# Low keys on both partition halves: a full-height second score matmul, and duplicated key loads as two DMAs of 64 rows

## Chip, cores and metric

The kernel runs on one core of one Trainium2 chip. The metric is the device time of one launch in microseconds. Shown are the median and the ends of three runs, and one further execution that the hardware profiler recorded.

## What is computed

One inference step of a two-layer streaming encoder, for a prompt of 1024 positions (one sequence) and for 8 x 16 sample positions that attend to cached keys and values. Layer 0 uses sliding-window attention with 4 key heads shared by 16 query heads, learned sinks and a T5 bias; layer 1 uses a band of 9 chunks of 64 positions, 16 heads, and a key and value projected once from the residual stream. Each attention is followed by an output projection, a normalisation, and a gated MLP with a causal convolution. The part that matters here is the attention over the prompt:

```python
def band_attend(q, k, v, qpos, kpos, bias, sinks, n_back):
    ...
    s = jnp.einsum('bqkgd,bskd->bkgqs', qg, k).astype(jnp.float32) * ATTN_SCALE
    s = s + bias.reshape(KV, G, Lq, Lk).astype(jnp.float32)
    ...
        p = jax.nn.softmax(s, axis=-1)
    ...
    o = jnp.einsum('bkgqs,bskd->bqkgd', p.astype(v.dtype), v)
```

Head dimension is 64, so one score has 64 products. Everything is float32.

## The kernel before

Nearly all matmuls run on pairs of numbers: a value is split into a high part, rounded to the matmul's input type, and a low part, the rest. A product is then formed as high x high + high x low + low x high. For the weight matmuls (the functions `mmT`, line 266, and `mmX`, line 278) that is three matmuls of 128 rows for each block.

The program is straight-line code: key and value projections, attention, output projection (`out_proj`) and MLP (`ffn`) for each of the two layers. Attention works through 16 heads (8 column blocks c of two halves a) and, for each head, four pairs g of query tiles with 128 queries each. `work` lists these 64 pairs. For each pair, `scores` forms the scores, `softmax` takes a minimum on VectorE (line 471) and an exponential on ScalarE (line 475), `weigh` transposes the probabilities on TensorE (line 533) and splits them (lines 538, 539), and `values` multiplies them with the values (line 552). These run one to three pairs apart, and between them stand blocks of the next query projection (`qblock`, line 266), steps of the adaptive-norm weights (`ada`, line 210, in layer 0) and the items of the sample positions (lines 619, 654). A scheduler orders the instructions of the five engines from its own model of time; each engine then takes its instructions in order. All DMAs are issued in order from SyncE's queue, SP.

A query tile holds 64 dimensions on 128 partitions: the high part on one half (r), the low part on the other. The high keys of a head (`khi[a]`, 64 rows of 1024 positions) lie on both halves, so that one matmul of 128 rows (line 505) gives high query x high key + low query x high key. The low keys (`klo`, one tile for both halves a) lie on one half only, and a second matmul of 64 rows (line 510) adds high query x low key into the same accumulator. In layer 0 a query tile sees 128 or 256 keys, in layer 1 128 to 640; over 512 they are split into two pieces. Over both layers there are 320 such pieces.

`kload(c, a)` brings the keys and values of a head from DRAM: line 433 fills both halves of `khi[a]` with one DMA whose source is read twice (a leading dimension of 2 with stride 0), line 434 brings the 64 low rows, line 435 the values. It is called 20 times: twice ahead of each layer's loop, and in `finish`, once a head's last values are formed, 14 times in layer 1 and twice in layer 0.

Buffers: `pts` is a ring of eight tiles for the split, transposed probabilities (four in X2, four in the weight slots 2 and 3). The weight slots are four pairs of tiles `wh`, `wl`; in attention the query weights use slots 0 and 1, and just ahead of it the projections use all four. `out_proj` loads its eight blocks of weights ahead, into the weight slots and into parts of the tile that held keys, values and queries (`x1att`), through two staging tiles `ws` (line 164), ScalarE (line 149) and GpSimd or VectorE (line 160).

Of the kernel before, what the change touches and what calls it, by code (L numbers as in the profile page):

```python
# [10 lines left out]
F32 = mybir.dt.float32  # L11
# [76 lines left out]
class Trunk:  # L88
# [249 lines left out]
    def attention(self, l, wk):  # L338
        nc, I = self.nc, self.I
# [4 lines left out]
        self.X1 = self.x1p.tile([128, 9216], F32R, name=f"x1att{l}", tag="x1")  # L344
        xa = Arena(self.X1)
        khi = [xa.take(1024) for _ in range(2)]
        klo = xa.take(1024)
        vst = [xa.take(1024).rearrange("p (k d) -> p k d", d=128) for _ in range(2)]
        qst = [[xa.take(1024) for _ in range(2)] for _ in range(2)]

        def qs(c, a, r, t0, n):
            if c == 7:
                return self.H[r, a, 0, t0 : t0 + n]
            return qst[c % 2][a][r, t0 : t0 + n]

        x2 = Arena(self.X2)
        pts = [(x2.take(512), x2.take(512)) for _ in range(4)]
        pts += [(w[:, 0:512], w[:, 512:1024]) for s in self.wslots[2:4] for w in s]
        pts = Ring(pts)
        fa = Arena(self.F)  # L360
        sKt = fa.take(2176)
# [28 lines left out]
        def head_of(c, a):  # L390
            return 8 * (c // 4) + 4 * a + c % 4 if l == 0 else 2 * c + a
# [24 lines left out]
        for p in range(2):  # L416
            t = sb.next()[:, 0:KS]
# [9 lines left out]
            sbt.append(t)  # L427

        def kload(c, a):
            r = slice(64 * a, 64 * a + 64)  # L430
            row = c * 128 + 64 * a
            kh, kl = kH[0, row : row + 64, :], kH[1, row : row + 64, :]
            nc.sync.dma_start(khi[a].bitcast(F32), bass.AP(kh.tensor, kh.offset, [[0, 2], [1024, 64], [1, 1024]]))
            nc.sync.dma_start(klo[r, :].bitcast(F32), kl)
            nc.sync.dma_start(
                vst[a].bitcast(F32), vH[:, 2 * c + a, :].rearrange("(k p) d -> p k d", p=128)
            )
# [29 lines left out]
        def softmax(pieces, p, n, sink, nm, rs):  # L467

            init = 3.0e38 if sink is None else sink
            for ps, b, c0, w in pieces:  # L470
                nc.vector.tensor_tensor_reduce(  # L471
                    out=p[:, c0 : c0 + w], in0=ps, in1=b, scale=1.0, scalar=init, op0=ALU.add, op1=ALU.min, accum_out=nm
                )
                init = nm
            nc.scalar.activation(p[:, 0:n], p[:, 0:n], AF.Exp, bias=nm, scale=-1.0, accum_out=rs)

        def scores(x):
            c, a, g = x.head.c, x.head.a, x.g
            hh = 2 * c + a
            h = head_of(c, a)  # L480
            r = slice(64 * a, 64 * a + 64)
            if g == 0:
                x.head.b = bias.next()
                nc.sync.dma_start(x.head.b, bass.AP(base.tensor, base.offset + h * HS + 127, [[EW - 1, 128], [1, W]]))
                nc.gpsimd.memset(x.head.b[0:64, W - 64 : W], BIG)  # L485
                nc.gpsimd.memset(x.head.b[64:128, 0:64], BIG)
            x.p = []
            for qi in (2 * g, 2 * g + 1):
                k0 = max(0, qi - back)
                n = (qi + 1 - k0) * 128  # L490
                p = pring.next()
                bo = W - n
                widths = [n] if n <= 512 else [n // 2, n // 2]
                pieces, c0 = [], 0
                for w in widths:
                    first = l == 1 or qi == 2 * g
                    if first:
                        s = self.bank(sbk.next())
                    o = s[:, 0:w] if first else s[:, 256 : 256 + w]
                    kc = slice(k0 * 128 + c0, k0 * 128 + c0 + w)  # L500
                    kw = {"skip_group_check": True} if l == 0 else {}
                    with ExitStack() as es:
                        if not first:
                            es.enter_context(self.tc.issue_after(lead))
                        mm = nc.tensor.matmul(  # L505
                            o, qs(c, a, slice(0, 128), qi * 128, 128), khi[a][:, kc], start=first, stop=False, **kw
                        )
                    if first:
                        lead = mm.ins
                    nc.tensor.matmul(o, qs(c, a, r, qi * 128, 128), klo[r, kc], start=False, stop=True, **kw)  # L510
                    pieces.append((o, x.head.b[:, bo + c0 : bo + c0 + w], c0, w))
                    c0 += w
                i = hh * 8 + qi
                nm = M[:, i : i + 1] if l == 0 else self.sm.next()[:, 0:1]
                softmax(pieces, p, n, self.sink[:, h : h + 1] if l == 0 else None, nm, L[:, i : i + 1])
                x.p.append((p, k0))
# [179 lines left out]
        def finish(i):  # L696
            x = work[i]
            values(x)
            if x.g == 3:
                c, a = x.head.c, x.head.a  # L700
                if l == 1 and c < 7:
                    kload(c + 1, a)
                elif l == 0 and c == 3:
                    kload(1, a)
            if i == 6 * 8 - 1:
                sums(0)

        for a in range(2):
            kload(0, a)
# [5 lines left out]
        for i, x in enumerate(work):  # L715
            scores(x)
            for c, bi in QAT.get(i, ()):
                if bi is None:
                    qload(c)
                else:  # L720
                    qblock(c, bi, qw[c])
            if i >= lw:
                weigh(work[i - lw])
            if i >= lag:
                finish(i - lag)
            self.step(BGA)
            if not self.bg and len(sbk.items) == 4:
                sbk.items = [0, 1, 2, 3, 4]
            for _ in range(ITEMS.count(i)):
                steps += items.pop(0)  # L730
            for _ in range(min(len(steps), 1 + (len(steps) > 4) + (len(steps) > 8))):
                steps.pop(0)()
# [616 lines left out]
```

## Time and profile before

| | us |
|---|---|
| median of 3 runs | 3238.45 |
| lowest, highest | 3228.12, 3243.93 |
| the profiled execution | 3225.61 |
| its span | 3223.7 |
| TensorE busy | 3004.9 (93%) |
| weight loads of TensorE | 2606.3 (81%) |
| VectorE busy | 1519.0 (47%) |
| ScalarE busy | 1137.0 (35%) |
| GpSimd busy | 830.6 (26%) |
| DMA, moved | 367.54 MB |

Times in the views count from the start of the span. PE is TensorE's matmul row, PEld its weight loads, DVE VectorE, ACT ScalarE, POOL GpSimd, SPq the queue of DMA issues. A row of the timeline gives start, duration, engine, line, operation, tiles, shape and count; in brackets the idle time of the engine ahead of it and what ended it ("issue" where the profile shows nothing that it waited for). A row of the chain gives start, duration and the piece of work on the path that ended last. PEclk is the granted clock of TensorE as a share of full speed.

The attention of layer 0 lies at about 125 to 435 us, that of layer 1 at about 1770 to 2190 us. The long stretches of `ffn` lie between and behind them.

### The profile page before, as it was taken

Reading aid. Unit: us, or ns where it says so; the run is one execution under the profiler, and the core shown is the slowest. Engines: PE = TensorE matmul, PEld = TensorE weight load, DVE = VectorE, ACT = ScalarE, POOL = GpSimd, SP = SyncE. Lnnn points to the kernel's source line nnn. Section 1 sums busy time; section 2 is a strip of 40 time slices with the busy share of each in tenths; the row PEclk is TensorE's granted clock in tenths of the full one; section 3 lists DMA queues with packets and bytes.
Section 4 is the critical chain, followed back from the end, with each engine's and each line's share of the span. In section 5 each row is a group of like instructions: output and inputs, shape, how many; then the busy total and the mean of one; then the engine's idle time right before and its main releaser. Section 6 shows DMA issues by size and latency. Waiting matters only on the chain.

```text
span 3223.7 us, 42690 instructions
## 1 busy us (share of the span) xinstructions
PE 3004.9 (93%) x16524; PEld 2606.3 (81%) x16524; DVE 1519.0 (47%) x3162; ACT 1137.0 (35%) x2400; POOL 830.6 (26%) x599
## 2 busy tenths in 40 slices
PE   7799976999999999998899999987699999999996
PEld 4676755888888888897899877755589999999996
DVE  4244556724444443458213545545662444444458
ACT  3254632432222222224335555542244222222224
POOL 2001202422222222254451000000242222222243
PEclk8898987999999999999999999977899999999999
DMA  7334467532222222223685245458531111111122
GB/s 287 126 113 143 142 161 153 196 128 74 79 77 87 87 82 85 83 85 126 225 272 170 89 120 156 131 150 185 126 133 42 46 40 48 41 40 40 40 72 81
DMA packets 226035, 367.54 MB, mean 114 GB/s; under 512 B 34448, under 2 KB 148944, under 8 KB 225448
## 3 DMA queue, kind: packets, MB, share of 16 engines
q1 hardware_dynamic: 225832, 364.81, 36.6%
q8 instruction: 130, 2.13, 0.3%
q14 instruction: 73, 0.60, 0.1%
HBM read 289.40 MB, written 84.79 MB: 116 GB/s over the span
## 4 chain that ended last, share of the span: by engine, by line
PE 71%; DMA 12%; DVE 7%; SPq 3%; POOL 2%; issue 2%; ACT 2%; DVEq 0%; ACTq 0%; POOLq 0%
PE PS L266 41%; PE PS L1057 15%; PE PS L552 3%; PE PS L510 3%; PE PS L210 3%; PE PS L533 2%; PE PS L278 2%; PE PS L505 2%; DMA x1att<-rD 1%; DMA F<-rD 1%; DMA F<-zd 1%; DMA ws<-in_wo_dram 1%; DMA X<-oT 1%; DMA oT<-F 1%; DMA F<-xd 1%
## 5 line engine op out<-in xcount | busy, mean ns | idle before, releaser
L266 PE MATMUL PS<-H,wh 128*128 128x384 f32 (+1 forms) x5472 | 1057.8, 341 | 0.3 <-DVE H L160 0.3
L266 PEld LDWEIGHTS PS<-H,wh 128*128 128x128 f32 x5472 | 973.2, 190 | 20.6 <-issue 9.1
L266 PE MATMUL PS<-H,wl 128*128 128x384 f32 (+1 forms) x2736 | 576.3, 348 | 41.7 <-DVE X L327 13.5
L986 DVE SCALAR_TENSOR_TENSOR F<-PS,F 128x256 f32<-128x256 f32 (+2 forms) x704 | 353.0, 512 | 532.9 <-ACT F L983 519.5
L160 POOL TENSOR_TENSOR wl<-ws,wh 128x1024 fp32r<-128x1024 f32 x167 | 407.4, 2445 | 741.5 <-ACT wh L149 722.3
L266 PEld LDWEIGHTS PS<-H,wl 128*128 128x128 f32 x2736 | 493.4, 192 | 84.8 <-issue 37.5
L1057 PE MATMUL PS<-wh,X 128*128 128x512 f32 x1584 | 466.8, 394 | 12.8 <-DVE acc L1048 4.3
L983 ACT ACTIVATE F<-PS,F 128x384 f32<-128x384 f32 x264 | 177.4, 672 | 756.7 <-PE PS L266 755.3
L1057 PEld LDWEIGHTS PS<-wh,X 128*128 128x128 f32 x1584 | 294.2, 188 | 75.5 <-issue 9.2
L1048 DVE TENSOR_TENSOR acc<-acc,PS 128x512 f32<-128x512 f32 x324 | 221.5, 686 | 273.1 <-PE PS L1057 272.1
L1032 POOL TENSOR_TENSOR F<-F 128x384 f32<-128x384 f32 x132 | 138.1, 1046 | 642.5 <-ACT F L1030 640.6
L1057 PE MATMUL PS<-wl,X 128*128 128x512 f32 x792 | 246.8, 393 | 0.0
L278 PE MATMUL PS<-wh,H 128*128 128x256 f32 (+1 forms) x1008 | 198.8, 327 | 35.8 <-DVE H L160 27.7
L149 ACT CAST wh<-ws 128x1024 fp32r<-128x1024 f32 x176 | 182.1, 1045 | 132.5 <-PE PS L1057 76.9
L278 PEld LDWEIGHTS PS<-wh,H 128*128 128x128 f32 x1008 | 154.8, 199 | 51.7 <-DVE H L160 29.3
L1057 PEld LDWEIGHTS PS<-wl,X 128*128 128x128 f32 x792 | 149.3, 189 | 33.0
L160 DVE TENSOR_TENSOR X<-F,X 128x384 fp32r<-128x384 f32 x132 | 116.8, 885 | 101.6 <-ACT X L149 101.1
L533 PE MATMUL PS<-C,F 128*128 128x128 f32 x720 | 127.9, 294 | 14.2 <-DVE X L539 10.3
L471 DVE CUSTOM_DVE_ANT_0 F<-PS,F,C 128x256 f32<-128x256 f32 (+3 forms) x208 | 98.1, 481 | 80.7 <-PE PS L510 63.1
L485 POOL MEMSET F<- 64x64 f32 x32 | 4.6, 144 | 470.2 <-DMA F<-skb 250.9
L160 POOL TENSOR_TENSOR H<-F,H 128x1024 fp32r<-128x1024 f32 x23 | 58.4, 2537 | 248.2 <-ACT H L149 155.4
L471 DVE CUSTOM_DVE_ANT_0 F<-PS,F 128x320 f32<-128x320 f32 (+5 forms) x144 | 67.7, 481 | 109.2 <-PE PS L533 67.1
(192 smaller groups left out, 3310.2 us busy)
## 6 DMA issues: line engine op xcount, KB each, us to landing
ws<-in_wup_dram SPq DMA_DIRECT2D x88, 512.0 KB
F<-in_adaw_dram SPq DMA_DIRECT2D x74, 512.0 KB
ws<-in_wdn_dram SPq DMA_DIRECT2D x44, 512.0 KB
ws<-in_adaw_dram SPq DMA_DIRECT2D x32, 512.0 KB
X<-oT SPq DMA_DIRECT2D x64, 256.0 KB
xd<-F SPq DMA_DIRECT2D x27, 512.0 KB
F<-xd SPq DMA_DIRECT2D x27, 512.0 KB
x1att<-kH SPq DMA_DIRECT2D x20, 512.0 KB
```

The costliest lines, as they stand in the source:

```text
L149: nc.scalar.copy(out, in_)
L160: self.eng(el).tensor_sub(lo, src, hi.bitcast(F32))
L210: nc.tensor.matmul(ps[32 * j : 32 * j + 32, :], self.cT[:, k * 32 : k * 32 + 32], w[:, j2 * 512 : j2 * 512 + 512], start=k == 0, stop=k == ...
L266: self.nc.tensor.matmul(out[:, 0:n], w[a][:, k * 128 : k * 128 + 128], H[:, p, k, s0 : s0 + n], start=i == 0, stop=i == 23)
L278: self.nc.tensor.matmul(out[:, 0:n], H[:, p, j * kn + k, t0 : t0 + 128], w[a][:, k * n : k * n + n], start=i == 0, stop=i == 23,)
L471: nc.vector.tensor_tensor_reduce(out=p[:, c0 : c0 + w], in0=ps, in1=b, scale=1.0, scalar=init, op0=ALU.add, op1=ALU.min, accum_out=nm)
L533: nc.tensor.transpose(t[:, m * 128 : m * 128 + 128], p[:, (kt - k0) * 128 : (kt - k0) * 128 + 128], self.ident)
L983: nc.scalar.activation(y, ps[:, off : off + 384], AF.Identity, bias=w(3), scale=w(2))
L986: nc.vector.scalar_tensor_tensor(o, u, w(i), o, op0=ALU.mult, op1=ALU.add)
L1032: nc.gpsimd.tensor_mul(a, y, ya[bi])
L1048: nc.vector.tensor_add(row[:, n], row[:, n], ps)
L1057: nc.tensor.matmul(ps, ac[m][p][:, cs], w[m][q][:, n], start=i == 0, stop=i == 5)
```

## The change

The low keys get a tile for each half a: the first stays where `klo` was, the second is the low tile of weight slot 3, which leaves the ring `pts`. Each tile holds the 64 rows twice, on both partition halves, like the high keys. The second score matmul takes the same 128-row query tile as the first, so it adds low query x low key as well. In `kload` every half of every key tile is a DMA of its own, from 64 rows to 64 partitions: four key DMAs per call instead of two, and 512 KB of low keys instead of 256 KB.

```diff
-        klo = xa.take(1024)
+        klo = [xa.take(1024), self.wslots[3][1]]
...
-        pts += [(w[:, 0:512], w[:, 512:1024]) for s in self.wslots[2:4] for w in s]
+        pts += [(w[:, 0:512], w[:, 512:1024]) for w in (*self.wslots[2], self.wslots[3][0])]
...
         def kload(c, a):
-            r = slice(64 * a, 64 * a + 64)
             row = c * 128 + 64 * a
             kh, kl = kH[0, row : row + 64, :], kH[1, row : row + 64, :]
-            nc.sync.dma_start(khi[a].bitcast(F32), bass.AP(kh.tensor, kh.offset, [[0, 2], [1024, 64], [1, 1024]]))
-            nc.sync.dma_start(klo[r, :].bitcast(F32), kl)
+            for t, k in ((khi[a], kh), (klo[a], kl)):
+                for b in range(2):
+                    nc.sync.dma_start(t[64 * b : 64 * b + 64, :].bitcast(F32), k)
...
+                q = qs(c, a, slice(0, 128), qi * 128, 128)
...
-                        mm = nc.tensor.matmul(
-                            o, qs(c, a, slice(0, 128), qi * 128, 128), khi[a][:, kc], start=first, stop=False, **kw
-                        )
+                        mm = nc.tensor.matmul(o, q, khi[a][:, kc], start=first, stop=False, **kw)
...
-                    nc.tensor.matmul(o, qs(c, a, r, qi * 128, 128), klo[r, kc], start=False, stop=True, **kw)
+                    nc.tensor.matmul(o, q, klo[a][:, kc], start=False, stop=True, **kw)
```

Two lines fewer stand in the changed file, so lines behind `kload` carry lower numbers there: the second score matmul is line 510 before and line 508 after, the transposes 533 and 531, the values 552 and 550, the output stores 567 and 565. Below, the shape at a row's end is the matmul's output.

TensorE late in layer 1, before (the two score matmuls are 505 and 510, between them transposes 533 and values 552):

```order
L505 MATMUL PS<-x1att_10403 128x320
L510 MATMUL PS<-x1att_10403 128x320
L266 MATMUL PS<-H,wh 128x384 x2
L505 MATMUL PS<-x1att_10403 128x320
L510 MATMUL PS<-x1att_10403 128x320
L533 MATMUL PS<-C,F 128x128 x4
L552 MATMUL PS<-wl,x1att_10403 128x128 x4
```

TensorE at about the same place of the changed program, for a head with a = 1:

```order
L505 MATMUL PS<-x1att_10411 128x320
L508 MATMUL PS<-wl,x1att_10411 128x320
L505 MATMUL PS<-x1att_10411 128x320
L508 MATMUL PS<-wl,x1att_10411 128x320
L266 MATMUL PS<-H,wh 128x384 x5
L505 MATMUL PS<-x1att_10411 128x320
L508 MATMUL PS<-wl,x1att_10411 128x320
```

The second score matmul stands where it stood, right behind the first; it now reads a weight slot (wl) as its keys. The counts of all other matmuls are the same, and most stand within a few places of where they stood.

SyncE's queue late in layer 1, before (433 and 434 are the key loads, 164 a weight block of the output projection, 567 the output stores, 582 the sums):

```order
L435 DMA x1att_10403<-vH_83 128x8x128
L567 DMA oT<-F 128x256
L582 DMA rD_89<-C 96x128
L433 DMA x1att_10403<-kH_79 128x1x1024
L434 DMA x1att_10403<-kH_79 64x1024
L484 DMA F<-skb 128x640
L164 DMA ws<-in_wo_dram 128x1024
```

The same place of the changed program (434 is now the one line of all key DMAs):

```order
L435 DMA x1att_10411<-vH_83 128x8x128
L565 DMA oT<-F 128x256
L434 DMA x1att_10411<-kH_79 64x1024 x2
L580 DMA rD_89<-C 96x128
L434 DMA x1att_10411<-kH_79 64x1024
L565 DMA oT<-F 128x256
L434 DMA x1att_10411<-kH_79 64x1024
L483 DMA F<-skb 128x640
L164 DMA ws<-in_wo_dram 128x1024
```

Four DMAs of 64 rows take the place of the broadcast DMA and the one of 64 rows, an output store moves in between, and the same weight block follows them.

SyncE's queue at the first key loads of layer 0, before (328 stores the values of the projection, 207 loads weights of the adaptive norm):

```order
L433 DMA x1att_273<-kH_78 128x1x1024
L328 DMA vH_82<-X_70 128x512
L434 DMA x1att_273<-kH_78 64x1024
L433 DMA x1att_273<-kH_78 128x1x1024
L434 DMA x1att_273<-kH_78 64x1024
L328 DMA vH_82<-X_70 128x512
L484 DMA F<-ska 128x256
L207 DMA ws<-in_adaw_dram 128x1024 x2
```

And after:

```order
L434 DMA x1att_273<-kH_78 64x1024
L328 DMA vH_82<-X_70 128x512
L434 DMA x1att_273<-kH_78 64x1024 x3
L328 DMA vH_82<-X_70 128x512
L434 DMA x1att_273<-kH_78 64x1024 x2
L483 DMA F<-ska 128x256
L207 DMA ws<-in_adaw_dram 128x1024
L328 DMA vH_82<-X_70 128x512
```

The six loads into `x1att` stand among the same value stores; the two low-key loads of a = 1, into the weight slot, come later, behind nearly all value stores.

More of the change, by code (lines that the diff above doesn't have):

```diff
@@ L480, in scores @@
             h = head_of(c, a)
-            r = slice(64 * a, 64 * a + 64)
             if g == 0:
```

## Prediction

> **What bounds the kernel now.** I read the busy time by stretch first, then the chain that ended last, then single rows of the attention stages. The columns of the first view are the stretch, its length, the busy time (and instructions) of TensorE, its weight loads, VectorE, ScalarE and GpSimd, the granted clock, the DMA share and GB/s.
>
> ```profile
> core 0: us, PE busy (x) PEld busy (x) DVE busy (x) ACT busy (x) POOL busy (x), PEclk, DMA share, GB/s
> 80.00:125.00 45.00, 28.75 (x196) 28.34 (x196) 3.63 (x10) 3.90 (x11) 1.36 (x5) 0.81 0.46 145
> 125.00:435.00 310.00, 302.14 (x1949) 227.24 (x1949) 151.82 (x517) 168.15 (x503) 35.01 (x46) 0.97 0.39 126
> 1770.00:2190.00 420.00, 396.12 (x2485) 306.11 (x2485) 217.92 (x691) 220.13 (x557) 27.82 (x38) 0.91 0.46 130
> by line: PE PS L266 40.6%; PE PS L1057 14.5%; PE PS L552 2.8%; PE PS L510 2.7%; PE PS L210 2.5%; PE PS L533 2.5%; PE PS L278 2.3%; issue 2.1%; PE PS L505 1.9%; DMA x1att<-rD 1.2%; DMA F<-rD 1.0%; DMA F<-zd 0.9%; DMA ws<-in_wo_dram 0.9%; DMA
> ```
>
> The change touches three stretches: the first key loads (80 to 125), the attention of layer 0 (to 435) and of layer 1 (1770 to 2190). In both attentions TensorE is busy for 97% and 94% of the time, VectorE and ScalarE for about half. TensorE sets the pace there, and its instructions are taken in order. The score matmuls L505 and L510 hold 4.6% of the chain, 148 us.
>
> **The score matmuls.** Each score piece of N keys is L505 on 128 rows, then L510 on 64 rows. The rows below (start, duration, engine; in brackets the idle time before) are two pieces of 320 keys, then 256, then 512.
>
> ```profile
> 1820.06 0.30 PE L505 MATMUL PS<-x1att 128*128 128x320 f32 x1
> 1820.30 0.18 PEld L510 LDWEIGHTS PS<-x1att 64*128 64x128 f32 x1 [0.16 <-issue]
> ...
> 1820.63 0.19 PEld L505 LDWEIGHTS PS<-x1att 128*128 128x128 f32 x1 [0.15 <-DVE wl L539]
> ...
> 1820.98 0.18 PEld L510 LDWEIGHTS PS<-x1att 64*128 64x128 f32 x1 [0.16 <-issue]
> ...
> 1821.31 0.42 PEld L533 LDWEIGHTS PS<-C,F 128*128 128x128 f32 x4 [0.15 <-issue]
> ...
> 283.80 0.28 PE L505 MATMUL PS<-x1att 128*128 128x256 f32 x1
> 284.01 0.38 PE L510 MATMUL PS<-x1att 64*128 64x256 f32 x1
> 284.32 0.39 PE L505 MATMUL PS<-x1att 128*128 128x256 f32 x1
> 284.64 0.38 PE L510 MATMUL PS<-x1att 64*128 64x256 f32 x1
> 284.95 0.33 PE L505 MATMUL PS<-x1att 128*128 128x128 f32 x1
> ...
> 2062.79 0.50 PE L505 MATMUL PS<-x1att 128*128 128x512 f32 x1
> 2063.22 0.50 PE L510 MATMUL PS<-x1att 64*128 64x512 f32 x1
> 2063.65 0.41 PE L505 MATMUL PS<-x1att 128*128 128x320 f32 x1
> ```
>
> Every weight load for L510, and the next load after it, begins only when the matmul ahead is over (0.15 to 0.16 us of idle load path). From start to start a piece takes 0.57 or 0.68 us at 320 keys (1820.06 to 1820.63 to 1821.31), 0.52 or 0.63 at 256, 0.86 at 512. Runs of 128-row matmuls do better. These are chain rows (start, time, matmuls):
>
> ```profile
> 1673.23 56.12 PE PS L278 x468
> 719.71 12.87 PE PS L266 x72
> 2433.09 4.11 PE PS L1057 x18
> ```
>
> L278 streams 256 columns, L266 384 and L1057 512, each with a fresh 128-row load per matmul. They take 0.120, 0.179 and 0.228 us apiece, so 320 columns take about 0.15 (an estimate between the first two). The new second matmul has 128 rows and the same query weights. A piece would then cost two such steps: 0.24 us at 256 (saves 0.28 to 0.39, I take 0.34), 0.30 at 320 (saves 0.27 to 0.38, I take 0.33), 0.46 at 512 (saves 0.40). Counts from the code: 128 pieces at 256, 128 at 320, 16 at 512, 16 at 384 and 32 at 128. For the last three together I take 0.30 each, near the lower rows. The sum is 128 x 0.34 + 128 x 0.33 + 64 x 0.30 = 105 us, with ends of 0.27 x 320 = 86 and 0.39 x 320 = 125.
>
> What of it is on the path: all 320 pieces cost about 0.62 us today, 198 us, and the chain holds 148 us of L505 and L510, three quarters. I take **79 us** (0.75 x 105). What is late next is VectorE and ScalarE, with 218 and 220 us of work in the 420 us of layer 1. They could still follow at 340 us, at two thirds busy, though each chain from score to softmax to transpose has to turn round faster.
>
> The Trainium skill ("TensorE: Matmul & The Clock Gate", Part 3, what overlaps and what doesn't) says that a weight load overlaps matmuls in flight only when its row group differs. By that rule a full-height load behind a full-height matmul would be as exposed as now and this term would be 0. This trace disagrees: the 468 full-height L278 pairs run at 0.120 us, not at the 0.31 us of the exposed rows.
>
> **The key loads.** Today L433 fills both halves of the high keys in one DMA and L434 follows. SyncE's queue, the chain, ScalarE and TensorE late in layer 1:
>
> ```profile
> 2092.59 0.52 SPq L433 DMA_DIRECT2D x1att<-kH  x1
> 2093.20 0.49 SPq L434 DMA_DIRECT2D x1att<-kH  x1
> 2095.44 0.34 SPq L164 DMA_DIRECT2D ws<-in_wo_dram  x1
> ...
> 2095.44 15.90 DMA ws<-in_wo_dram
> ...
> 2111.36 1.04 ACT L149 CAST x1att<-ws 128x1024 fp32r<-128x1024 f32 x1 [10.48 <-DMA ws<-in_wo_dram]
> ...
> 2113.67 1.54 PE L533 MATMUL PS<-C,F 128*128 128x128 f32 x6 [10.03 <-DVE X L539]
> ...
> 1418.68 3.33 DMA ws<-in_wdn_dram
> ```
>
> A 512 KB weight load takes 3.33 us when alone, and 15.90 us when it is issued 2.85 us behind L433. ScalarE waits 10.48 us for it in front of its queue, and TensorE stands 10.03 us. The other TensorE stalls of over 1.3 us that I find behind an L433, with one DMA of the first of them and two stretches at half clock:
>
> ```profile
> 99.19 0.74 PE L278 MATMUL PS<-wh,H 128*128 128x256 f32 x4 [2.77 <-DVE X L327]
> 117.30 2.90 PE L266 MATMUL PS<-H,wl 128*128 128x384 f32 x8 [13.47 <-DVE X L327]
> 100.50 15.71 DMA vH<-X
> 273.66 1.92 PE L210 MATMUL PS<-ws,C 128*32 128x512 f32 x4 [1.35 <-DMA ws<-in_adaw_dram]
> 288.09 1.94 PE L210 MATMUL PS<-ws,C 128*32 128x512 f32 x8 [2.38 <-DMA ws<-in_adaw_dram]
> 1917.49 1.22 PE L552 MATMUL PS<-X,x1att 128*128 128x256 f32 x4 [2.57 <-ACT F L564]
> 2073.84 1.66 PE L654 MATMUL PS<-F 128*32 128x128 f32 x24 [5.12 <-ACT F L564]
> 1920.00:1930.00 10.00, 10.00 (x39) 7.65 (x39) 3.91 (x15) 3.40 (x8) 0.00 (x0) 0.51 0.42 115
> 2120.00:2130.00 10.00, 10.00 (x58) 6.87 (x57) 3.82 (x15) 3.62 (x8) 2.37 (x1) 0.50 0.50 143
> ```
>
> The seven waits add up to 37.7 us, and after a stall the clock stands at half: these two stretches alone lose 5 us each. That is 48 us. The changed kernel fills each half with a DMA of 64 rows, in the form that L434 has now. No row shows such a load with nothing ahead of it; between nothing gone (0) and all of it gone (48) I take **41 us**, about 1 us left of each of the seven waits, because the nearest row is the 3.33 us of a DMA spread over all partitions. The Trainium skill ("DMA: Bandwidth & Descriptors", "Why a DMA increments its semaphore by 16 and not by 1") says that a DMA runs on the largest number of engines up to 16 that divides the slowest dimension of both sides: 2 for the old form, with its leading 2, and 16 for 64 rows. No view here shows the engines of one DMA.
>
> **What is added.** Two more issues per call, 40 in all, at the 0.49 us of the L434 row: 20 us of SyncE's queue, hidden where that queue waits for other engines; uncovered it would be 20. Low keys of the odd heads move to a weight slot that the value projection reads until it ends; those loads stand behind its last store in the order, and their head is the second to run. The ring of transposed probabilities loses one of eight tiles; a pair uses at most three and two pairs are live, so seven suffice. For all of these together I take 4 us, between 0 and 20.
>
> **The sum.** The profiled execution took 3225.61 us (span 3223.7). 3225.6 - 79 - 41 + 4 = 3109.6. The median shown, 3238.45, is 12.8 above that execution, so the forecast is **3122 us**.
>
> **Rivals.**
> - The other engines take over. Faster scores only make TensorE wait for the softmax in layer 1; for it speaks the length of that chain of engines, against it the half-idle VectorE and ScalarE. Half of the score term is left, 40: 3238 - 40 - 41 + 4 = 3161.
> - The loads stay slow, so that the change doesn't do this part. For it: no row shows a 64-row load alone. Against: only DMAs behind the broadcast form are slow. 3238 - 79 + 4 = 3163.
> - The full-height load is not hidden behind the first matmul (the skill's rule above gives this). Against: the L278 row. 3238 - 41 + 4 = 3201.
> - Slower: the reload becomes the stall. Five DMAs per reload instead of three stand in one in-order queue ahead of the output stores and the wo loads; if each of the 16 reloads inside the loops costs TensorE the 10.03 us of the row above, 160 us come and 79 go: 3238 + 81 = 3319. It decides once a reload costs more than 79 / 16 = 4.9 us of TensorE. Against: the new reload moves 1 MB of keys where 768 KB went, in more pieces but not in the slow form.
>
> **How the numbers follow.** Chances: forecast 0.72 (its own range 3060 to 3150: score term 63 to 125, loads 30 to 48), other engines 0.11, slow loads 0.09, exposed load 0.05, slower 0.03. The range 3060 to 3180 takes in the first three and leaves out the last two and the tails. Half a per cent, 16 us, is about what a measurement of this kernel can tell from no change: faster by more than that 0.94, within it 0.03, slower 0.03.
>
> **What would show it.** The second score matmul has 128 rows and no idle load path ahead of it, a piece of 256 takes about 0.24 us, and layer 1's attention shrinks from 420 us to some 340. DMAs behind a key load land in under 7 us, and the 13.47, 10.03 and 5.12 us stalls are gone. If TensorE's share in the attention falls well below 90% with waits on VectorE or ScalarE, the first rival holds; if the stalls stay, the second; if pieces still take 0.6 us, the third. I would be wrong altogether if TensorE waited for keys at each new head.

## The result, and the profile after

| | us |
|---|---|
| before, median of 4 runs in the same session | 3235.70 (3228.12 to 3243.93) |
| changed, median of 4 runs | 3066.59 (3062.19 to 3071.40) |
| ratio | 0.9477, 95% interval 0.9449 to 0.9506 |
| span of the profiled execution, before and changed | 3223.7 and 3063.9 |

The change takes off 169 us; the forecast was 116 (3238 to 3122), and its range ended at 3060. The 160 us of span can be placed by landmarks: the first and the last score matmul of each layer, and three rows of the chain of waits, which are the first row of 72 matmuls in the MLP of layer 0 (at 719.71 us before, 661.73 changed), the value projection of layer 1 (L278 x468) and the first long block of layer 1's MLP (L266 x264, at 2379.59 and 2218.40). Where such a landmark came earlier or later by more than the one ahead of it, the stretch between them gained or lost:

| stretch | before, us | changed, us | difference |
|---|---|---|---|
| start to the first score of layer 0 | 131.4 | 110.7 | -20.7 |
| attention of layer 0 | 289.8 | 248.4 | -41.5 |
| output projection of layer 0, to the MLP | 298.4 | 302.7 | +4.2 |
| MLP of layer 0 and key projection of layer 1 | 953.5 | 938.8 | -14.8 |
| value projection of layer 1, to its first score | 88.0 | 90.0 | +1.9 |
| attention of layer 1 | 415.5 | 317.6 | -97.9 |
| output projection of layer 1, to the MLP | 202.9 | 210.4 | +7.5 |
| MLP of layer 1 | 844.1 | 845.5 | +1.4 |

The timeline of TensorE in layer 1, changed kernel (start, duration, engine, line, shapes): a piece of 512 keys, two pieces of 320, and the weight loads of the first. The second score matmul is now L508.

```profile
1760.67 0.50 PE L505 MATMUL PS<-x1att 128*128 128x512 f32 x1
1761.02 0.40 PE L508 MATMUL PS<-x1att 128*128 128x512 f32 x1
1761.26 0.56 PE L550 MATMUL PS<-wl,x1att 128*128 128x128 f32 x4
...
1769.98 0.36 PE L505 MATMUL PS<-x1att 128*128 128x320 f32 x1
1770.18 0.31 PE L508 MATMUL PS<-x1att 128*128 128x320 f32 x1
1770.33 0.30 PE L505 MATMUL PS<-x1att 128*128 128x320 f32 x1
1770.47 0.31 PE L508 MATMUL PS<-x1att 128*128 128x320 f32 x1
1770.61 0.82 PE L531 MATMUL PS<-C,F 128*128 128x128 f32 x6
...
1760.67 0.19 PEld L505 LDWEIGHTS PS<-x1att 128*128 128x128 f32 x1
1760.78 0.19 PEld L508 LDWEIGHTS PS<-x1att 128*128 128x128 f32 x1
```

The bracket with 0.16 us of idle load path is gone, and the load for L508 begins 0.24 us before its matmul. From start to start a piece of 320 keys takes 0.28 to 0.35 us (1770.33 to 1770.61, 1769.98 to 1770.33) where it took 0.57 to 0.68; a piece of 512 takes 0.59 where it took 0.86. L508 itself takes 0.14 to 0.15 us at 320, as the prediction's estimate between two chain rows had it.

The stretches, changed kernel (stretch, length, then busy time of TensorE, its weight loads, VectorE, ScalarE, GpSimd, then granted clock, DMA share, GB/s):

```profile
80.00:125.00 45.00, 45.00 (x313) 42.43 (x311) 11.78 (x34) 13.99 (x38) 2.71 (x6) 1.00 0.70 208
110.00:360.00 250.00, 244.03 (x1817) 200.05 (x1817) 139.87 (x487) 158.30 (x487) 35.17 (x46) 0.98 0.47 150
1690.00:2008.00 318.00, 310.21 (x2415) 278.27 (x2416) 213.31 (x676) 214.27 (x548) 27.98 (x38) 0.98 0.64 178
```

The kernel before, for its own attention of layer 1:

```profile
1761.00:2177.00 416.00, 394.57 (x2416) 306.21 (x2416) 216.28 (x679) 218.36 (x551) 27.82 (x38) 0.91 0.45 127
```

Four things are to be read here. In 80 to 125 us TensorE was busy for 28.75 us, now for all 45. In layer 1 TensorE is still busy for 97.5% (310.21 of 318), with VectorE and ScalarE at two thirds: it still sets the pace. Its idle time there fell from 21.4 us to 7.8. And the granted clock rose from 0.91 to 0.98, so that part of the 84 us of busy time that went is probably clock and not shorter work; run 2 below puts a number on it.

Chain rows of the changed kernel (start, time, matmuls or transfer):

```profile
1506.70 93.78 PE PS L266 x541
1600.48 56.12 PE PS L278 x468
1953.11 6.93 DMA ws<-in_wo_dram
```

The key projection of layer 1 is one unbroken row of 541 matmuls. A weight block issued right behind a key load lands in 6.93 us, where it took 15.90.

### The profile page after: what moved, and what is told of

Its sections match the earlier page's. It is cut to its first block, busy times and chain, and to the rows that moved or that the text cites. A ratio compares the mean times of both kernels' runs of the same rounds, so it can differ in the third digit from the quotient of the medians.

```text
span 3063.9 us, 42731 instructions
## 1 busy us (share of the span) xinstructions
PE 2865.6 (94%) x16524; PEld 2555.5 (83%) x16524; DVE 1515.7 (49%) x3162; ACT 1131.2 (37%) x2400; POOL 835.1 (27%) x599
## 4 chain that ended last, share of the span: by engine, by line
PE 77%; DVE 8%; DMA 7%; SPq 3%; ACT 2%; POOL 2%; issue 2%; DVEq 0%; ACTq 0%; POOLq 0%
PE PS L266 45%; PE PS L1055 15%; PE PS L278 3%; PE PS L550 3%; PE PS L210 3%; PE PS L531 2%; SPq L924 2%; DMA X<-oT 2%; PE PS L505 2%; PE PS L508 1%; SPq L929 1%; PE PS L652 1%; POOL wl L160 1%; DMA F<-in_xrow_dram 1%; DVE F L945 1%
## 5 line engine op out<-in xcount | busy, mean ns | idle before, releaser
L266 PE MATMUL PS<-H,wh 128*128 128x384 f32 (+1 forms) x5472 | 1049.2, 339 | 0.3 <-DVE H L160 0.3
L266 PEld LDWEIGHTS PS<-H,wh 128*128 128x128 f32 x5472 | 967.7, 189 | 17.1 <-issue 8.2
L266 PE MATMUL PS<-H,wl 128*128 128x384 f32 (+1 forms) x2736 | 567.4, 344 | 24.3 <-DVE C L814 9.5
L266 PEld LDWEIGHTS PS<-H,wl 128*128 128x128 f32 x2736 | 488.4, 190 | 63.7 <-issue 27.7
L278 PE MATMUL PS<-wh,H 128*128 128x256 f32 (+1 forms) x1008 | 195.5, 323 | 38.7 <-DVE H L160 36.2
L278 PEld LDWEIGHTS PS<-wh,H 128*128 128x128 f32 x1008 | 152.7, 196 | 53.8 <-DVE H L160 37.4
L531 PE MATMUL PS<-C,F 128*128 128x128 f32 x720 | 120.5, 282 | 5.4 <-DVE X L537 3.4
L1028 ACT ACTIVATE F<-F 128x384 f32<-128x384 f32 x132 | 69.2, 524 | 143.8 <-DVE F L984 129.2
L278 PE MATMUL PS<-x1att,H 128*128 128x512 f32 x432 | 112.2, 407 | 0.0
```

Of the source, the lines that this page charges most:

```text
L266: self.nc.tensor.matmul(out[:, 0:n], w[a][:, k * 128 : k * 128 + 128], H[:, p, k, s0 : s0 + n], start=i == 0, stop=i == 23)
L278: self.nc.tensor.matmul(out[:, 0:n], H[:, p, j * kn + k, t0 : t0 + 128], w[a][:, k * n : k * n + n], start=i == 0, stop=i == 23,)
L531: nc.tensor.transpose(t[:, m * 128 : m * 128 + 128], p[:, (kt - k0) * 128 : (kt - k0) * 128 + 128], self.ident)
```

## The experiments

All seven were timed against the kernel before, on one chip for each group of runs: runs 1 to 4 stood beside a median of 3231.36 us (3225.28 to 3241.09), runs 5 to 7 beside 3232.95 (3213.57 to 3242.27). "Scores" means the full-height second matmul with its duplicated low keys, "loads" the high keys by two DMAs of 64 rows.

| | median, us | ratio to before, 95% interval |
|---|---|---|
| 1 scores only | 3177.59 | 0.9823 (0.9787 to 0.9859) |
| 2 loads only | 3151.55 | 0.9750 (0.9719 to 0.9781) |
| 3 scores, high keys in 62 + 2 rows | 3165.74 | 0.9794 (0.9770 to 0.9819) |
| 4 loads, half-height matmuls grouped | 3126.47 | 0.9672 (0.9643 to 0.9701) |
| 5 before, ring of seven | 3243.28 | 1.0027 (1.0010 to 1.0044) |
| 6 scores, all keys by the broadcast form | 3323.11 | 1.0270 (1.0244 to 1.0297) |
| 7 changed, gate rows split | 3067.64 | 0.9480 (0.9454 to 0.9506) |

**1. Scores only**: the changed kernel with the old form for the high keys. The question is whether the gain of the scores stands by itself.

```diff
-            for t, k in ((khi[a], kh), (klo[a], kl)):
-                for b in range(2):
-                    nc.sync.dma_start(t[64 * b : 64 * b + 64, :].bitcast(F32), k)
+            nc.sync.dma_start(khi[a].bitcast(F32), bass.AP(kh.tensor, kh.offset, [[0, 2], [1024, 64], [1, 1024]]))
+            for b in range(2):
+                nc.sync.dma_start(klo[a][64 * b : 64 * b + 64, :].bitcast(F32), kl)
```

> The changed kernel, but the high keys come again by one broadcast DMA to both halves; the low keys by two DMAs of 64 rows. Theory (two separate gains, scores and loads): the score pieces run at about 0.32 us for 256 keys and 0.35 us for 320, as in the changed kernel, the stalls behind the broadcast loads stay (first score at about 131 us), and the time is about 3236 - 95 = 3141 us (3125 to 3160). Rival (a faster TensorE only runs into the slow loads): the score rows are as fast, but less than 60 us are gained, 3176 us or more.

Measured: 3177.59, 54 us below the kernel before and 111 above the changed one, so the rival holds. Layer 1 and rows of the chain, this kernel:

```profile
1733.00:2118.00 385.00, 326.44 (x2420) 291.85 (x2421) 215.37 (x679) 214.94 (x551) 27.95 (x38) 0.91 0.53 147
```

```profile
1757.05 14.88 DMA x1att<-kH
...
1980.41 17.48 DMA oT<-F
...
2005.03 15.76 DMA ws<-in_wo_dram
```

What TensorE waited for in layer 1, this kernel (line, what ended the wait, us in total, times, longest; L531 are the transposes, L550 the values, L652 an item of the sample positions):

```profile
PE PS L531 <- DVE wl L537: 11.7, 1, 11.7
PE PS L531 <- DVE X L537: 11.6, 1, 11.6
PE PS L550 <- ACT F L562: 11.2, 4, 5.2
PE PS L652 <- DMA F<-in_cvB_dram: 11.2, 2, 10.9
PE PS L505 <- DMA x1att<-kH: 5.0, 2, 3.2
```

TensorE's busy time fell by 68 us, but its idle time rose from 21.4 to 58.6 (385 less 326.44), and the clock stayed at 0.91. Little of this is a wait for the keys themselves (5.0 us at L505 and 4.4 at the second matmul); most stands, as in the kernel before, at transposes, values and items whose own inputs or buffers came late. The chain runs through slow transfers of 15 to 17 us (key loads, output stores, weight blocks), so these waits are put down to them; that was not tried for each. Faster scores do not shorten such transfers, and TensorE waits more.

**2. Loads only**: the kernel before with one edit.

```diff
-            nc.sync.dma_start(khi[a].bitcast(F32), bass.AP(kh.tensor, kh.offset, [[0, 2], [1024, 64], [1, 1024]]))
+            for b in range(2):
+                nc.sync.dma_start(khi[a][64 * b : 64 * b + 64, :].bitcast(F32), kh)
```

> The kernel before, with the high keys by two DMAs of 64 rows and nothing else changed. Theory: score pieces stay at about 0.61 and 0.66 us, the first score moves from 131 to about 111 us, the 17.5 us transfer of zd in the key projection of layer 1 and the 10.03 and 5.12 us stalls go, and the time falls by 65 to 80 us, to 3156 to 3171. Rival (the loads are worth what the prediction put on them): 41 us, 3195.

Measured: 3151.55, 80 us below the kernel before, 4 us past the end of the expected range and twice what the prediction gave the loads. Layer 1, this kernel:

```profile
1729.00:2106.00 377.00, 373.24 (x2416) 291.01 (x2416) 216.21 (x680) 218.48 (x552) 27.91 (x38) 0.98 0.49 140
```

The same 2416 matmuls, in the same form as before, are busy for 373.24 us instead of 394.57, at a clock of 0.98 instead of 0.91: 21 us. That the clock did this is read from the two figures standing side by side; their ratio alone would give 28 (an estimate: 394.57 x (1 - 0.91/0.98)). The idle time goes from 21.4 to 3.8: 18 us. By the landmarks, attention of layer 1 gives 39 of this profile's 70 us of span, the start 20, and the stretch from the last score of layer 0 to the value projection of layer 1, with the key projection in it, another 16.

Layer 0 shows that the clock can also go the other way. Its attention, first the kernel before, then this one, then a stretch near this one's end:

```profile
131.40:421.30 289.90, 284.12 (x1810) 212.48 (x1808) 141.79 (x485) 160.68 (x484) 35.01 (x46) 0.97 0.39 125
111.60:403.90 292.30, 290.70 (x1808) 216.75 (x1807) 142.61 (x485) 161.52 (x486) 35.04 (x46) 0.94 0.38 124
390.00:404.00 14.00, 14.00 (x78) 8.98 (x78) 6.85 (x29) 6.44 (x22) 0.00 (x0) 0.50 0.06 20
```

TensorE's idle time fell there from 5.8 us to 1.6, as the loads would have it, but the clock fell too, and the busy time rose by 6.6 us. For 14 us at the end TensorE was busy all the time at half clock, and its longest wait in the 24 us ahead of that was 0.55 us. Why is not shown.

**3. Is it the double read or the number of rows?** The changed kernel, with each half of the high keys as 62 and 2 rows, so that no source is read twice within a DMA.

```diff
-            for t, k in ((khi[a], kh), (klo[a], kl)):
-                for b in range(2):
-                    nc.sync.dma_start(t[64 * b : 64 * b + 64, :].bitcast(F32), k)
+            for b in range(2):
+                for i, j in ((0, 62), (62, 64)):
+                    nc.sync.dma_start(khi[a][64 * b + i : 64 * b + j, :].bitcast(F32), kh[i:j, :])
+                nc.sync.dma_start(klo[a][64 * b : 64 * b + 64, :].bitcast(F32), kl)
```

> The changed kernel, but each half of the high keys comes as a DMA of 62 rows and one of 2 rows; no source is read twice within a DMA. Theory (the number of rows sets on how many engines a DMA runs; 62 = 2 x 31 gives few): DMAs behind a key load take over 10 us again, the stalls return, and the time is near that of the run with broadcast high keys, 3125 to 3170. Rival (reading the source twice is what was slow): as fast as the changed kernel, 3060 to 3080, give or take 40 more issues.

Measured: 3165.74, within 12 us of scores only and 99 above the changed kernel, inside the theory's range. Rows of its chain:

```profile
1573.71 14.39 DMA F<-zd
...
1803.28 13.81 DMA x1att<-kH
```

A load of 62 rows is nearly as slow as the old broadcast (13.81 against 14.88 in run 1), and a transfer in the key projection takes 14.39 us (17.50 before). So a load can be slow with no source that is read twice; the two more issues per call, of about half a microsecond each, do not explain transfers of 14 us. The Trainium skill ("DMA: Bandwidth & Descriptors", "Why a DMA increments its semaphore by 16 and not by 1") gives a rule that covers both: a DMA runs on the largest number of engines up to 16 that divides the slowest dimension of both sides, 2 for a leading 2 and 2 for 62 rows. The times of both runs agree with it; no view here shows the engines of one DMA.

**4. Is a 64-row load always exposed, or only the change of height?** Run 2, with the order high, high, low, low in tiles of two pieces (47 of 64 then stand so on TensorE), where it was high, low, high, low.

```diff
-                    nc.tensor.matmul(o, qs(c, a, r, qi * 128, 128), klo[r, kc], start=False, stop=True, **kw)
+                    second.append((o, kc))
...
+                with ExitStack() as es:
+                    if len(second) > 1:
+                        es.enter_context(self.tc.issue_after(mm.ins))
+                    for o, kc in second:
+                        nc.tensor.matmul(o, qs(c, a, r, qi * 128, 128), klo[r, kc], start=False, stop=True, **kw)
```

> The loads-only kernel, with the two pieces of a 640-key tile in the order high, high, low, low, so that 47 of 64 such tiles have their two 64-row matmuls next to each other. Theory A (the exposed load belongs to the change between 128 and 64 rows): two changes fewer in each of the 47 tiles, 94 x about 0.17 = 16 us less than the loads-only run. Theory B (every 64-row load and the load after it are exposed, whatever stands ahead): the same time as the loads-only run within 5 us, and two 64-row matmuls in a row still 0.33 us apart.

Measured: 3126.47, 25 us below loads only; theory A forecast 16, theory B none. Layer 1, two half-height matmuls in a row and their loads, this kernel:

```profile
1719.00:2077.00 358.00, 354.12 (x2416) 283.67 (x2416) 214.99 (x677) 217.05 (x550) 27.88 (x38) 0.99 0.52 147
```

```profile
1860.30 0.56 PE L518 MATMUL PS<-x1att 64*128 64x320 f32 x2
1860.79 0.66 PE L539 MATMUL PS<-C,F 128*128 128x128 f32 x4
...
1860.30 0.29 PEld L518 LDWEIGHTS PS<-x1att 64*128 64x128 f32 x2 [0.17 <-issue]
1860.78 0.42 PEld L539 LDWEIGHTS PS<-C,F 128*128 128x128 f32 x4 [0.19 <-issue]
```

The two half-height matmuls take 0.49 us together (1860.30 to 1860.79), and the chain of the kernel before has 0.34 for one:

```profile
2151.55 0.34 PE PS L510
```

So the second costs some 0.15, no more than a full-height step. There is one idle gap going in and one coming out. What is exposed is the change between 128 and 64 rows, not the half-height load. TensorE's busy time in layer 1 fell by 19 us (373.24 to 354.12), near theory A's 16. Some 10 us more of the two profiles' difference arise ahead of layer 1, where no tile has two pieces, and were not traced to a cause; executions of one kernel differ by as much (3143 to 3159 for run 2).

**5. The lost buffer**: the kernel before with seven tiles in the ring of probabilities.

```diff
-        pts += [(w[:, 0:512], w[:, 512:1024]) for s in self.wslots[2:4] for w in s]
+        pts += [(w[:, 0:512], w[:, 512:1024]) for w in (*self.wslots[2], self.wslots[3][0])]
```

> The kernel before with one edit: the ring of split, transposed probabilities holds seven tiles instead of eight, as in the changed kernel. The prediction put this at nothing: a pair uses at most three tiles and two pairs are live. Expected within 0.5% of the kernel before, 3215 to 3248 us. Rival: the eighth tile lets the splits of a third pair run ahead and hides waits of TensorE on VectorE; then the time rises by more than 16 us, above 3248, and the change would have gained that much more without it.

Measured: 1.0027 of before, 3 to 14 us by the interval. Not nothing, but within the half per cent that was expected.

**6. The slower rival**: the changed kernel with the high and the low keys each by one broadcast DMA, so that a reload has two slow loads and no fast one.

```diff
             for t, k in ((khi[a], kh), (klo[a], kl)):
-                for b in range(2):
-                    nc.sync.dma_start(t[64 * b : 64 * b + 64, :].bitcast(F32), k)
+                nc.sync.dma_start(t.bitcast(F32), bass.AP(k.tensor, k.offset, [[0, 2], [1024, 64], [1, 1024]]))
```

> The changed kernel, but the high and the low keys of a head are each filled by one DMA whose source is read twice (two slow loads per reload instead of none). With one such load per reload the time was 3177.6, 111 above the changed kernel. Theory: a slow load is about 15 us of a few engines' time, so the second adds its own 15 us behind the first, a reload then takes some 30 us, and TensorE waits for keys at most heads of layer 1: 3230 to 3320, which is the prediction's slower rival (a reload that costs TensorE over 4.9 us). Rival: the two slow loads run side by side, and the reload takes about 15 us as with one: 3170 to 3200.

Measured: 3323.11, 257 us above the changed kernel and 2.7% slower than before, although its score matmuls are full height; the theory's range ended at 3320. Layer 1, its chain, one wait of TensorE, and SyncE's queue (here L507 is the second score matmul, L433 the key load and L564 an output store):

```profile
1771.00:2263.00 492.00, 337.12 (x2418) 300.35 (x2419) 215.96 (x678) 216.41 (x550) 27.91 (x38) 0.82 0.38 114
...
1794.44 23.56 DMA x1att<-kH
...
1886.72 17.07 DMA oT<-F
...
2009.00 23.62 DMA wl<-kH
```

```profile
2021.18 0.30 PE L504 MATMUL PS<-x1att 128*128 128x128 f32 x1
2032.67 0.48 PE L507 MATMUL PS<-wl,x1att 128*128 128x128 f32 x1 [11.19 <-DMA wl<-kH]
...
1793.83 1.09 SPq L433 DMA_DIRECT2D x1att<-kH  x2
1795.84 6.91 SPq L564 DMA_DIRECT2D oT<-F  x1
...
1816.09 10.21 SPq L433 DMA_DIRECT2D wl<-kH  x1
```

Two slow loads do not run side by side: the pair takes 23 to 24 us where one takes 15, though not the 30 of one after the other. SyncE's queue stands behind them (10.21 us for one issue, 0.5 usually), with the output stores in it, and TensorE waits for keys at a second score matmul (11.19 us). Its idle time in layer 1 is 154.9 us (492 less 337.12), against 21.4 before.

**7. The gate rows** of the sample positions have a source with a leading dimension of 8; here each of the eight goes by itself.

```diff
-        nc.sync.dma_start(self.gateS, bass.AP(g.tensor, g.offset + D, [[D, 8], [0, 16], [1, D]]))
+        for s in range(8):
+            nc.sync.dma_start(self.gateS[16 * s : 16 * s + 16, :], bass.AP(g.tensor, g.offset + D + s * D, [[0, 16], [1, D]]))
```

> The changed kernel with the gate of the sample positions (line 791: one DMA whose source has a leading dimension of 8, four times in the program) loaded as eight DMAs of 16 partitions each. In the chain of the changed kernel this DMA takes 11.60 us at 379.70, ahead of the loads of the attention's output. Theory: a leading dimension of 8 uses half of the engines, so that this load delays those behind it, and part of the roughly 15 us that the two output projections gave back is won: 3050 to 3062. Rival: the output projection is bound by its own many small loads, and seven more issues each time cost as much as they win: 3062 to 3075.

Measured: 3067.64, level with the changed kernel and in the rival's range. In layer 0 the transfer is shorter, first the changed kernel's chain, then this one's:

```profile
379.70 11.60 DMA F<-gd
...
397.84 10.64 DMA X<-oT
```

```profile
377.29 6.53 DMA F<-gd
...
397.02 8.47 DMA X<-oT
```

The transfer gave up 5 us, and the load behind it in the chain began only 0.8 us earlier (397.84 to 397.02); counted from the last score of layer 0 (359.1 and 357.6) it began 0.6 us later. Whether the output projection waits for its other small loads anyway, or the seven issues more cost what was won, the run does not separate. None of the seven runs beats the changed kernel.

## Why the prediction was right in direction and too small in size

**What bounds the kernel** was right. TensorE sets the pace in both attentions before and after, and the first rival, that VectorE and ScalarE take over, did not come: at 67% busy in layer 1 they still leave TensorE its 97.5%.

**The score term** (79 us) was nearly right, and that is in part luck, since two errors cancel. From run 2 to the changed kernel it is 85 us (3151.55 to 3066.59), the lost buffer included. Summed over all 640 score matmuls from start to next start, with idle time taken out, the pieces went from 209 us to 113 (from 205 in run 2): 92 to 96, not 105, because the first matmul of a piece still takes 0.20 us (median), not 0.12 at 256 keys and 0.15 at 320. But nearly all of it lay on the path, not three quarters: in run 2, with the loads out of the way, TensorE was busy for 99% of layer 1's attention (373.24 of 377), and the chain's share of the two lines was a poor measure of that. The rival of the exposed full-height load fell, and with it the Trainium skill's sentence ("TensorE: Matmul & The Clock Gate", Part 3, what overlaps and what doesn't): full-height L508 runs behind full-height L505 at 0.14 to 0.15 us, its load in the shadow of the matmul ahead; none of the 320 loads for L508 has idle load path ahead of it, where 299 of the 320 for L510 had.

**The load term** (41 us) is the step that failed by its size. It is worth 80 alone (run 2) and 111 once the scores are fast (run 1 against the changed kernel). The waits that it did count were priced about rightly: 17.7 of its 37.7 us lie in layer 1, where run 2 took off 18 us of idle time, and 16.2 at the first key loads, where it took off 20. Three things were left out.

First, a place. The seven waits were taken from behind reloads in the attention and at the first key loads, and the key projection of layer 1 was not searched. It has the same stall, in the kernel before (queue, then chain):

```profile
1578.90 0.53 SPq L433 DMA_DIRECT2D x1att<-kH  x1
...
1580.03 0.82 SPq L433 DMA_DIRECT2D x1att<-kH  x1
1580.89 8.84 SPq L299 DMA_DIRECT2D kH<-X  x1
...
1592.01 17.50 DMA F<-zd
```

Two broadcast loads, then an issue that takes 8.84 us and a transfer of 17.50 on the chain. TensorE over the key projection, before and in run 2:

```profile
1554.80:1673.20 118.40, 109.78 (x627) 109.03 (x626) 14.35 (x30) 34.93 (x75) 69.86 (x36) 0.96 0.77 256
1534.60:1640.20 105.60, 105.60 (x626) 105.60 (x625) 14.45 (x30) 35.26 (x75) 69.97 (x37) 1.00 0.90 295
```

That is 12.8 us, 8.6 of them idle time and 4.2 longer busy time at a clock of 0.96; with the MLP ahead of it the stretch gave 14 us in run 2 and 15 in the whole change.

Second, the clock. The prediction counted two stretches at half clock, 10 us. The mean of 0.91 over the attention of layer 1 was a row in its own first fence; in run 2 it is 0.98, and the same matmuls are busy for 21 us less. That a stall is followed by half clock, as the prediction read it, fits layer 1, but is not all: run 2's layer 0 has half clock in a stretch without a stall, and run 1 has the same mean of 0.91 in layer 1 with 58.6 us of idle time instead of 21.4.

Third, the two parts are not a sum. The prediction subtracted both from one profile. Scores alone are worth 54 us and loads alone 80, which makes 134, and together they are worth 165 to 169 (by the median of before in either session): with slow loads, TensorE saves 68 us of work in layer 1 (run 1) and gives 37 back in waiting. So some 31 us come only when both parts are there. In the order loads, then scores, the second part takes them, and the terms are 80 and 85.

**The marks it gave** came out so: 128 rows and no idle load path, yes; 0.24 us for a piece of 256, not quite: 0.32 by the medians, of which L508 takes the 0.12 forecast and L505 0.20; the stalls of 13.47 and 5.12 us, gone, and of the 10.03 a wait of 3.1 us is left at the transposes; DMAs behind a key load under 7 us, just (6.93); layer 1's attention at 340 us, less still, 318.

**What is added** (4 us) is about 12 in the landmarks: 4.2 and 7.5 us in the two output projections. The lost buffer, put at nothing, cost 3 to 14 us in the kernel before. For the output projection of layer 1 the queue shows a reason. The first loads of the attention's output, changed kernel and before:

```profile
2016.60 6.22 SPq L677 DMA_DIRECT2D oSD<-C  x2
...
2024.74 0.62 SPq L924 DMA_DIRECT2D X<-oT  x1
```

```profile
2184.36 1.31 SPq L926 DMA_DIRECT2D X<-oT  x2
```

In the changed program they stand behind the last stores of the sample positions and go out 16.7 us after the last score (2008.0); before it was 7.6 us (2176.7). That this order costs the 7.5 us is read from the rows; it was not tried.

**The slower rival** was a real mechanism with about its price, for another load form: with two broadcast loads per reload (run 6) the time is 3323, the rival had 3319. The rival put 10.03 us on each reload; run 6 has 133 us more idle time in layer 1 than the kernel before, 9.5 for each of its 14 reloads. What kept the change from it is the 64-row form, not the size of the reload, which moves 1 MB of keys in both. The slow-loads rival fell with run 2.

**The bounds.** The load term was bounded at 48 us by the stalls found in one reading. That is no upper bound: it leaves out the stalls not found, and what a faster TensorE would have waited in addition. A time near the low end of the range was the result.

## What to carry to other kernels

A slow DMA in a shared queue costs more than the waits that stand right behind it: look for its shadow at every place where the same line is issued, and look at the mean granted clock of the stretch as well as at its idle time, though the idle time alone does not say what the clock will be. Two gains on one path, faster work and faster loads for it, are to be worked out one after the other, the second from what the first leaves, since either alone can turn into waiting. Where a matmul of 64 rows stands between matmuls of 128, price the change of height (here about 0.3 us a piece) and fill the height, or group the half-height ones.

## What the runs showed of the hardware

- A DMA of 62 rows delays what follows it by 14 us, about as the broadcast from a leading dimension of 2 does (15 us); with loads of 64 rows ahead of it, a weight block landed in 6.93 us. Two slow loads together take 23 to 24 us.
- The change between 128-row and 64-row matmuls leaves the load path idle for 0.16 to 0.19 us each way; a second 64-row matmul behind the first costs about 0.15 us. The Trainium skill ("TensorEngine Tiling (Array Packing)", Key Properties) says that a change of tiling mode drains TensorE; run 4 agrees, if a 64-row load counts as another mode, and puts the price beside it.
- With 2416 matmuls of the same form, the granted clock over the attention of layer 1 went from 0.91 to 0.98 when the idle time fell from 21.4 to 3.8 us of some 400 (run 2). The sum of idle time does not set it: run 1 has 0.91 with 58.6 us of idle time, and in the attention of layer 0 run 2 has less idle time than the kernel before (1.6 against 5.8 us) and a lower clock (0.94 against 0.97).
